# First layer of a two-block network: the pool's columns ahead of the recurrence, and the inverse in one pass over eight chunks

## The chip, the cores and the metric

The kernel runs on one core of a Trainium2 chip. The metric is the device time of one execution in microseconds (us). The engines are PE (TensorE, matmuls; PEld is its weight load), DVE (VectorE), ACT (ScalarE), POOL (GpSimd) and SP (SyncE, which issues most of the DMAs).

## The reference

Two blocks of a network over 256 tokens (and 256 context tokens) of width 2048. The change lies in layer 0 of the first block, where latent and context tokens, 512 rows in all, pass one projection `w_in` and are split: a pooling part, three vectors r, k, v for a recurrence with 16 heads of 64 in both directions, two small inputs for decay and a, and a gate.

```python
def wkv7_scan(state, inputs, reverse):
    def step(S, xs):
        r, w, k, v, a, b = xs
        sa = jnp.einsum('bhvk,bhk->bhv', S, a)
        S = S * w[:, :, None, :] + sa[..., None] * b[:, :, None, :] + v[..., None] * k[:, :, None, :]
        return S, jnp.einsum('bhvk,bhk->bhv', S, r)
...
def even_mixer(hl, hc, w_in, w_out, pool_w, pool_scale, ...):
    al, rl, kl, vl, wdl, adl, gl = split_even(hl @ w_in)
    ac, rc, kc, vc, wdc, adc, gc = split_even(hc @ w_in)
    for d, reverse in enumerate((False, True)):
        in_c = rwkv_dir_inputs(rc, kc, vc, wdc[..., d, :], adc[..., d, :], *dir_p, reverse)
        in_l = rwkv_dir_inputs(rl, kl, vl, wdl[..., d, :], adl[..., d, :], *dir_p, reverse)
        s_ctx, y_c = wkv7_scan(s0, in_c, reverse)
        _, y_l = wkv7_scan(s_ctx, in_l, reverse)
        outs_l.append(rwkv_readout(y_l, in_l, r_k, gn_g[d], gn_b[d]))
        ...
    ol = (outs_l[0] + outs_l[1]).astype(hl.dtype)
    yl = (jnp.concatenate([multiscale_pool(al, pool_w, pool_scale), ol], -1) * jax.nn.silu(gl)) @ w_out
```

The kernel computes the recurrence in chunks of 64 tokens. In each chunk the dependence of the tokens on each other is a triangular 64x64 system, whose inverse is found by doubling (five levels) and two refining steps; then a chain over the eight chunks carries the state.

## The kernel before

**Layer 0 in three kinds of work.** The *dense* work is `hX @ w_in`, in columns of 128 output features: 48 columns, each of 16 blocks of 128 inputs, each block a triple of matmuls 128x512 (L486 high part by high part, L487 high by low, L488 low by high), since float32 is split into two parts. `atoms` (L480) issues a column one triple at a time. Its weights come in two pieces of 512 KB a column (`need`, L835; `stream`, L466), each split in two halves into `whi` (ACT, L187) and `wlo` (DVE, L188). A column is one of r, k, v of a head pair (`rkv`), a gate (`gate`) or half of a pool group (`pool`). `poolmix` (L564) multiplies the pooled features by small weights (L571). *Side* work of the same queue is `mod` (L346), the modulation vectors, with four matmuls in a go at L369.

The *inverse*: there are 16 units, 8 head pairs p times 2 directions d. `wkv_prep` (L577) makes a unit's inputs. `wkv_half(u, g)` (L660) does chunks 4g to 4g+3 of both heads: masked copies S (the tile called STK in the code), the A matmuls (L692), DVE's masking of their result (L693, L701, L702), the subtraction at L695 and a cast on ACT (AT16, L697), and then steps of the form "eight 64x64 matmuls into the bank iv (`units`, L708), then one DVE operation out of that bank": x (L720, L746), t (L737, L750), y (L739, L752), each of 128x256. It also makes the transposed rows BT, UV, ZV (L724 to L734).

The *chain*: `wkv_chain(u, g)` (L756) goes through four chunks in three steps each: L770 on PE, R on DVE (L772); L776 on PE, UV on ACT (L777); L780 on PE, ZV on DVE (L783), with L784 and L785 on PE into the bank yb. `wkv_read` (L795) normalises the result, with the sums at L798 and L805.

**What sets the order.** PE's order is the order of the code (it is set by hand there); the other engines' order is a scheduler's, which takes the inverse's operations with priority 100 and the chain's with 60. `merge` (L911) writes the code order: each round takes one step of the inverse of one half, 0.75 steps of the chain of the half before, one step of prep and read, and then `fill`: as many dense triples (0.64 each by the planner's own unit) as keep the remaining dense work even over the remaining steps (`left`, `steps`, 575 in all). A unit goes through two merges: the inverse of its second half beside the chain of its first, and the inverse of the next unit's first half beside the chain of its second. `filler` (L869) hands out the columns in order, one entry of mod after nine triples. In the last unit, out-projection columns take the place of the dense ones.

## Time and profile before

| | us |
|---|---|
| time, median of 3 runs | 3622.39 |
| lowest and highest | 3620.04, 3637.42 |
| the profiled execution's own time | 3619.65 |
| its span in the profile | 3617.8 |
| PE busy in it | 3478.3 |
| DVE busy | 2240.6 |
| ACT busy | 1606.1 |

The mean granted clock of TensorE is 0.987 of its full 2.4 GHz. Layer 0's stage runs from about 299 to 1592 us. "Busy" on PE counts each matmul until its modelled end, and matmuls overlap, so the distance between two starts tells more of what one costs than its duration. An idle time in brackets, as in "[1.16 <-DVE R L772]", is the time in which the engine did nothing before this instruction, with what ended it.

### The profile page before, as it was taken

How to read it: one execution, taken by the hardware profiler on the slowest of the kernel's cores; microseconds unless marked ns; L12 is line 12 of the kernel's file. 1: busy time of each engine (PE TensorE's matmuls, PEld its weight loads, DVE VectorE, ACT ScalarE, POOL GpSimd, SP SyncE). 2: the span in 40 equal slices, each digit the busy share in tenths (PEclk: the TensorE clock that was granted, in tenths of full speed). 3: DMA queues.
4: the chain of work that ended last, by engine and by line, in shares of the span. 5: the costliest groups of instructions: out<-in, count | busy, mean ns of one | idle time of the engine just before them, and what ended most of it. 6: DMA issues, size and time to landing. Idle time of an engine off the chain costs nothing.

```text
span 3617.8 us, 56804 instructions
## 1 busy us (share of the span) xinstructions
PE 3478.3 (96%) x22385; PEld 2678.4 (74%) x22385; DVE 2240.6 (62%) x4180; ACT 1606.1 (44%) x2680; POOL 83.3 (2%) x168
## 2 busy tenths in 40 slices
PE   6999999999999999999999999999999999999998
PEld 4576666666666666678788887777888888888886
DVE  4253666777776777843656667766654566666544
ACT  3244344444444444431545555364444544444433
POOL 1000000000000000100000000000000000000000
PEclk9999999999999999999999999999999999999999
DMA  9976433344343344443444456454665566666654
GB/s 312 311 260 182 138 109 116 115 128 122 106 134 116 112 127 120 125 151 110 131 122 128 138 178 208 129 139 117 184 180 164 181 189 190 190 189 191 201 190 162
DMA packets 655652, 578.57 MB, mean 160 GB/s; under 512 B 24891, under 2 KB 498415, under 8 KB 655386
## 3 DMA queue, kind: packets, MB, share of 16 engines
q1 hardware_dynamic: 627008, 538.86, 49.9%
q10 hardware_dynamic: 24474, 29.09, 2.4%
q0 software_dynamic: 3904, 7.01, 0.7%
q8 instruction: 175, 2.87, 0.3%
q14 instruction: 91, 0.75, 0.1%
HBM read 547.32 MB, written 27.56 MB: 159 GB/s over the span
## 4 chain that ended last, share of the span: by engine, by line
issue 58%; PE 17%; DVE 3%; ACT 2%; DMA 1%; POOL 0%; ACTq 0%; POOLq 0%; SPq 0%; DVEq 0%
PE acc L486 3%; PE iv L708 3%; PE acc L487 2%; PE acc L488 2%; DMA raw<-ev_w_in 1%; PE acc L369 1%; PE ch L776 1%; PE ch L780 1%; PE sc L692 1%; PE ch L770 1%; PE yb L784 1%; PE yb L785 0%; DVE S L701 0%; ACT whi L187 0%; PE sc L724 0%
## 5 line engine op out<-in xcount | busy, mean ns | idle before, releaser
L188 DVE TENSOR_TENSOR wlo<-raw,whi 128x1024 fp32r<-128x1024 f32 (+1 forms) x857 | 928.2, 1088 | 813.2 <-ACT whi L187 806.7
L187 ACT CAST whi<-raw 128x1024 fp32r<-128x1024 f32 (+1 forms) x857 | 799.6, 940 | 1051.3 <-PE acc L207 212.2
L207 PE MATMUL acc<-A,whi 128*128 128x512 f32 x1488 | 531.6, 398 | 3.9 <-DVE A L1000 2.8
L208 PE MATMUL acc<-A,wlo 128*128 128x256 f32 x1488 | 424.2, 285 | 0.8 <-DVE wlo L188 0.8
L486 PE MATMUL acc<-A,whi 128*128 128x512 f32 x768 | 359.2, 468 | 22.8 <-ACT ev L497 14.2
L207 PEld LDWEIGHTS acc<-A,whi 128*128 128x128 f32 x1488 | 278.5, 187 | 68.3 <-DVE A L1000 3.1
L487 PE MATMUL acc<-B,whi 128*128 128x512 f32 x768 | 303.3, 395 | 0.0
L488 PE MATMUL acc<-A,wlo 128*128 128x512 f32 x768 | 302.0, 393 | 0.0
L208 PEld LDWEIGHTS acc<-A,wlo 128*128 128x128 f32 x1488 | 281.1, 189 | 5.1 <-DVE wlo L188 1.8
L207 PE MATMUL iv<-A,whi 128*128 128x512 f32 x736 | 257.5, 391 | 0.0
L208 PE MATMUL iv<-A,wlo 128*128 128x256 f32 x736 | 206.3, 280 | 1.0 <-DVE wlo L188 1.0
L486 PEld LDWEIGHTS acc<-A,whi 128*128 128x128 f32 x768 | 145.8, 190 | 81.9 <-issue 32.3
L488 PEld LDWEIGHTS acc<-A,wlo 128*128 128x128 f32 x768 | 144.8, 189 | 33.3
L487 PEld LDWEIGHTS acc<-B,whi 128*128 128x128 f32 x768 | 146.3, 191 | 22.0 <-issue 9.6
L207 PEld LDWEIGHTS iv<-A,whi 128*128 128x128 f32 x736 | 137.7, 187 | 30.3
L208 PEld LDWEIGHTS iv<-A,wlo 128*128 128x128 f32 x736 | 139.1, 189 | 1.5 <-DVE wlo L188 1.5
L720 DVE TENSOR_TENSOR x<-iv,k 128x256 f16<-128x256 f32 x160 | 67.4, 421 | 90.3 <-PE iv L708 88.4
L777 ACT COPY UV<-ch 64x128 f32<-64x128 f32 x128 | 33.3, 260 | 186.6 <-PE ch L776 182.0
L708 PEld LDWEIGHTS <-at 64*64 64x64 f16 x1536 | 40.4, 108 | 91.5 <-issue 75.6
L708 PEld LDWEIGHTS <-y 64*64 64x64 f16 x1536 | 40.1, 108 | 82.4 <-issue 50.6
L737 DVE TENSOR_TENSOR t<-iv,t 128x256 f16<-128x256 f32 x128 | 54.0, 422 | 48.2 <-PE iv L708 46.0
L776 PE MATMUL ch<-R,Y 128*128 128x128 f32 x256 | 63.3, 330 | 14.2 <-DVE R L772 14.0
(1540 smaller groups left out, 7136.3 us busy)
## 6 DMA issues: line engine op xcount, KB each, us to landing
raw<-w_gate_up SPq DMA_DIRECT2D x176, 512.0 KB, 4.7
raw<-mod_w SPq DMA_DIRECT2D x128, 512.0 KB, 4.0
raw<-ev_w_in SPq DMA_DIRECT2D x100, 512.0 KB, 4.6
raw<-w_down SPq DMA_DIRECT2D x88, 512.0 KB, 4.9
raw<-od_w_in SPq DMA_DIRECT2D x80, 512.0 KB, 3.7
raw<-w_in SPq DMA_DIRECT2D x80, 512.0 KB, 4.0
raw<-w_xkv SPq DMA_DIRECT2D x64, 512.0 KB, 6.6
A<-mod_w SPq DMA_DIRECT2D x64, 512.0 KB, 5.9
```

Of the source, the lines that this page charges most:

```text
L187: nc.scalar.copy(hi[:, q], raw[:, q])
L188: nc.vector.tensor_sub(lo[:, q], raw[:, q], hi[:, q].bitcast(F32))
L207: s.nc.tensor.matmul(acc, hi, x.rearrange("p a t -> p (a t)"), start=start, stop=False)
L208: s.nc.tensor.matmul(acc[:, 0:256], lo, x[:, 0], start=False, stop=stop)
L369: nc.tensor.matmul(acc[32 * q:32 * q + 32], s.SC[:, 2 * k:2 * k + 32], pair[q // 2][:, q % 2], start=k < 4, stop=k >= 12, tile_position=(0 ...
L486: s.nc.tensor.matmul(acc, hi[:, k], hX[kx], start=kx == 0, stop=False)
L487: s.nc.tensor.matmul(acc, hi[:, k], lX[kx], start=False, stop=False)
L488: s.nc.tensor.matmul(acc, lo[:, k], hX[kx], start=False, stop=kx == 15)
L708: nc.tensor.matmul(ps[hs[h], c], l(hs[h], c), r(hs[h], c), start=True, stop=True)
L720: tt(X16, px, b4(s.lv[d][l]), MUL)
L737: tt(T16 if l < 5 else T32, pt, T16, ADD)
L776: nc.tensor.matmul(pr[:, 128:256], fl(Y32[:, b:b + 2]), R1, start=True, stop=True)
```

## The change

**The pool first, in full pieces.** `rkv(0)` and then, for the four pool groups, two pool columns, two gates and the poolmix are queued first: 19 dense columns, with no `mod` among them. What of them is not used up in the first unit's prep is drained in one go before the first inverse, with pieces of 512 KB as before. 29 columns are left (`later`): r, k, v of the other head pairs and eight gates.

**Smaller pieces after that.** The room for weights is shared from then on: `small_stream` brings each column in four pieces of 256 KB (`kper` 4), through two raw halves and two halves each of `whi` and `wlo`, unsplit. The other three raw tiles hold mod's two pieces and the inverse's AT and T32; the other pair of `whi` and `wlo` holds S of every second unit (`s.S2`).

**The inverse over eight chunks.** `wkv_inv(u, e)` replaces the two `wkv_half`: each call of `units` is sixteen 64x64 matmuls (L741), each DVE operation out of it 128x512 (x L748, L756; T, Y L749, L753, L758). The masking is done for each half (L726, L730, L731), S only on its 64x256 part and AB over all 128 partitions, so that the fill of AB's lower part on POOL is gone. `wkv_rows` holds the transposes.

**The chain as the frame.** `wkv_chain` has 24 steps for a unit; `merge` takes one chain step in a round, 0.75 steps of the next unit's inverse, the prep of the unit after that (two units ahead) and the read of the one before, and then dense triples, over 18 + 24 x 15 steps. The read has two empty steps instead of six. The sum of both directions is taken up in prep (L675 to L677) instead of the read.

```diff
+    def small_stream(s, srcs, raws, his, los):
+
+        nc, loaded, got = s.nc, [0], {}
+
+        def get(i):
+            while loaded[0] < min(i + 3, len(srcs)):
+                j = loaded[0]
+                if j >= 2:
+                    split(j - 2)
+                nc.sync.dma_start(raws[j % 2], srcs[j])
+                loaded[0] += 1
+            for j in range(i, min(i + 2, len(srcs))):
+                split(j)
+            return got[i]
+
+        def split(j):
+            if j in got:
+                return
+            hi, lo = got[j] = his[j % 2], los[j % 2]
+            nc.scalar.copy(hi, raws[j % 2])
+            nc.vector.tensor_sub(lo, raws[j % 2], hi.bitcast(F32))
+        return get
+
...
-        for q in range(2):
+        for q in range(16 // s.kper):
             hi, lo = s.wget(i + q)
-            for k in range(8):
-                kx = 8 * q + k
+            for k in range(s.kper):
+                kx = s.kper * q + k
...
-        nc.vector.tensor_tensor(u.OUT, ps, V, MUL)
+        if d == 0:
+            nc.vector.tensor_tensor(u.OUT, ps, V, MUL)
+        else:
+            rk = s.T("tb", [P, 512])
+            nc.vector.tensor_tensor(rk, ps, V, MUL)
+            nc.vector.tensor_tensor(u.OUT, u.OUT, rk, ADD)
...
+        for g in range(2):
+            cs = slice(4 * g, 4 * g + 4)
+            pss = []
+            for h in range(2):
+                ps = s.PS("sc", (P, 4, 2, C))
+                for c in range(4):
+                    nc.tensor.matmul(ps[:, c], fl(u.BK)[:, 4 * g + c], u.S[g][:, c, :, h], start=True, stop=True)
+                tt(AT[hs[h], cs], ps[0:64, :, 0], b4(mk[0:64, 0:64], 64), MUL)
+                pss.append(ps)
+            yield 1
+            for h, ps in enumerate(pss):
+                tt(u.S[g][osd[h], :, 0, h], ps[64:128, :, 0], b4(mk[64:128, 0:64], 64), MUL)
+                tt(u.AB[g][:, :, h], ps[:, :, 1], b4(mk[:, 64:128], P), MUL)
+        tt(AT, AT, b8(s.id64), SUB)
+        AT16 = s.T("inv", [P, NCH, C], F16)
         nc.scalar.copy(AT16, AT)
...
         def units(l, r):
-            ps = s.PS("iv", (P, 4, C))
-            for c in range(4):
+            ps = s.PS("iv", (P, NCH, C))
+            for c in range(NCH):
                 for h in range(2):
                     nc.tensor.matmul(ps[hs[h], c], l(hs[h], c), r(hs[h], c), start=True, stop=True)
             return ps
...
+            tt(X16, px, b8(s.lv[d][l]), MUL)
...
+    def wkv_rows(s, u, g):
+
+        nc, hs, osd, C = s.nc, s.hs, s.osd, CH
+        fl = lambda t: t.rearrange("p c a t -> p c (a t)")
+        UV, ZV, BT = (s.T("%s%d" % (n, g), [P, 4, 2, C]) for n in ("UV", "ZV", "BT"))
...
+        ps = s.PS("sc", (P, 4, 128))
+        for c in range(4):
+            nc.tensor.transpose(ps[:, c], fl(u.BH[g])[:, c], s.ident)
+        nc.scalar.copy(fl(BT), ps)
+        u.h[g] = (UV, ZV, BT)
+
+    def wkv_chain(s, u, nxt, before):
+
...
+            if g == 0:
+                for x in before:
+                    for _ in x:
+                        pass
...
+            if g == 0 and nxt is not None:
+                s.wkv_rows(nxt, 0)
...
-        for _ in range(6):
+        for _ in range(2):
...
         nc.vector.tensor_tensor(OUT, OUT, YS, ADD)
-        if d == 0:
-            s.fwd = OUT
-        else:
-            nc.vector.tensor_tensor(OUT, OUT, s.fwd, ADD)
+        if d == 1:
+            s.await_gate(8 + p)
...
+        s.kper = 8
         rkv(0)
-        for p in range(8):
-            if p < 7:
-                rkv(p + 1)
-            if p in (2, 4, 6):
...
-        mods = [s.mod(0, 8, 12), s.mod(1, 0, 12)]
...
+        for g in range(4):
+            pool(g)
+            gate(2 * g)
+            gate(2 * g + 1)
+            jobs.append(s.l0_poolmix(g))
+        dense, dsrcs = jobs[:], srcs[:]
+        del jobs[:], srcs[:]
+
+        def later():
+            s.kper = 4
+            rkv(1)
+            for p in range(2, 8):
+                rkv(p)
+                gate(6 + p)
+            gate(14)
+            gate(15)
...
-                    if n % 9 == 0:
+                    if n * 80 // 464 > (n - 1) * 80 // 464:
...
-        steps = [575.0]
+        steps = [18.0 + 24 * 15]
...
         def merge(a, b, side):
-            na, nb, done = 16.0, 12.0, 0.0
...
+            due = 0.25
+            while a is not None or b is not None:
+                due += 0.75 if b is not None else 1.0
+                if a is not None and due >= 1.0:
+                    due -= 1.0
                     with s.prio(100):
-                        w = next(a, s)
-                    a, more = (a, True) if w is not s else (None, more)
-                    w = 1.0 if w is s else w
...
+                        if next(a, None) is None:
+                            a = None
+                if b is not None:
                     with s.prio(60):
-                        b, more = (b, True) if next(b, s) is not s else (None, more)
...
-                steps[0] = max(steps[0] - w, 1.0)
-                fill(w * left[0] / steps[0])
+                steps[0] = max(steps[0] - 1.0, 1.0)
+                fill(left[0] / steps[0])
...
         cur, pg = prep(0)
         for _ in pg:
             fill(1.5)
-        merge(s.wkv_half(cur, 0), None, [])
+        for _ in F:
+            pass
+
+        later()
+        raw = [s.T("raw", [P, 1024], bufs=s.nraw) for _ in range(4)]
+        r2 = raw[2].rearrange("p (n k c) -> p n k c", n=2, k=4)
+        s.AT, s.T32 = [raw[3][:, i * 512:(i + 1) * 512].rearrange("p (c t) -> p c t", c=NCH) for i in range(2)]
+        wh = [s.T(t, [P, 2, 4, 128], F32R, bufs=s.nhi) for t in ("whi", "wlo")]
+        s.S2 = [s.T(t, [P, 4, 2, 2, CH], bufs=s.nhi) for t in ("whi", "wlo")]
+        s.wget = s.small_stream(srcs, [r2[:, 0], r2[:, 1]], [wh[0][:, 0], wh[0][:, 1]], [wh[1][:, 0], wh[1][:, 1]])
+        F = filler([r.rearrange("p (k c) -> p k c", k=2) for r in raw[0:2]])
+        credit[0], left[0] = 0.0, 29 * 16 * 0.64 + 16 * (4 * 0.6 + 0.9)
+        nxt, pg = prep(1)
+        merge(s.wkv_inv(cur, 1), None, [pg])
+        s.wkv_rows(cur, 0)
         rg = []
         for n in range(16):
-            nxt, pg = prep(n + 1) if n < 15 else (None, iter(()))
-            merge(s.wkv_half(cur, 1), s.wkv_chain(cur, 0), rg + [pg])
+            s.wkv_rows(cur, 1)
+            nx2, pg = prep(n + 2) if n < 14 else (None, iter(()))
             if n == 15:
                 for _ in F:
                     pass
                 s.out0 = F = s.l0_out_n(0)
-                credit[0], left[0], steps[0] = 0.0, 18, 14.0
-            merge(s.wkv_half(nxt, 0) if nxt else None, s.wkv_chain(cur, 1), [])
+                credit[0], left[0], steps[0] = 0.0, 26, 24.0
+            merge(s.wkv_inv(nxt, n % 2) if nxt else None, s.wkv_chain(cur, nxt, rg), rg + [pg])
             rg = [s.wkv_read(cur)]
-            cur = nxt
+            cur, nxt = nxt, nx2
         for _ in rg[0]:
             fill(1.3)
```

What stands in a row on the engines, before and after. First PE in the steady middle of the stage, before: two rounds of the inverse, with the names iv<-t,at for x's matmuls, iv<-x,y and iv<-y,x for those of t and y. A row of L708 stands for eight such pairs of weight load and matmul, the rest of which are left out.

```order
L486 MATMUL acc<-A_1572,whi 128x512
L487 MATMUL acc<-B_1580,whi 128x512
L488 MATMUL acc<-A_1572,wlo 128x512
L708 LDWEIGHTS at_11856
L708 MATMUL iv<-t_11894,at_11856 64x64
...
L770 MATMUL ch<-ZV_11364,S_11354 128x128
L486 MATMUL acc<-A_1572,whi 128x512
L487 MATMUL acc<-B_1580,whi 128x512
L488 MATMUL acc<-A_1572,wlo 128x512
L486 MATMUL acc<-A_1573,whi 128x512
...
L708 LDWEIGHTS y_11895
L708 MATMUL iv<-x_11896,y_11895 64x64
```

After, the same kind of place; L741 is the inverse's line now, L819 to L824 the third step of the chain, and a row of L741 stands for sixteen pairs.

```order
L509 MATMUL acc<-A_1571,whi 128x512
L510 MATMUL acc<-B_1579,whi 128x512
L511 MATMUL acc<-A_1571,wlo 128x512
L369 MATMUL acc<-raw,SC 32x512 x4
L741 LDWEIGHTS T_12125
L741 MATMUL iv<-Y_12126,T_12125 64x64
...
L741 LDWEIGHTS Y_12126
L741 MATMUL iv<-T_12125,Y_12126 64x64
...
L819 MATMUL ch<-UV_11560,BT_11562 128x128
L823 MATMUL yb<-S_11134,ZV_11561 128x128
L824 MATMUL yb<-AB_11150,UV_11560 128x128
L509 MATMUL acc<-A_1571,whi 128x512
```

What moved: a round of the inverse has twice the matmuls, and the stretches of chain and dense work between rounds are no longer in the middle of four chunks.

Second, DVE at the head of an inverse, before: after the A matmuls the two AT parts (L693), S (L701), AB (L702), the subtraction (L695), then the chain's R (L772).

```order
L693 TENSOR_TENSOR AT<-sc,k_65 64x256
L701 TENSOR_TENSOR S_8902<-sc,k_65 64x8x64
L693 TENSOR_TENSOR AT<-sc,k_65 64x256
L702 TENSOR_TENSOR AB_8914<-sc,k_65 64x4x64
L695 TENSOR_TENSOR AT<-AT,id_83 128x256
L701 TENSOR_TENSOR S_8902<-sc,k_65 64x8x64
L702 TENSOR_TENSOR AB_8914<-sc,k_65 64x4x64
L716 TENSOR_TENSOR y_8988<-at_8954,k_1528 128x256
L772 TENSOR_TENSOR R_8961<-ch,k_65 128x128
L715 TENSOR_TENSOR t_8987<-iv,k_1528 128x256
```

After, with AT in a tile named raw (L726), S (L730) and AB (L731), for the second half of the unit; between the first half's such rows and these the chain's ZV (L822) now has its place.

```order
L822 SCALAR_TENSOR_TENSOR ZV_5807<-ZV_5807,We,ch 64x64 x2
L726 TENSOR_TENSOR raw<-sc,k_65 64x256
L730 TENSOR_TENSOR S_6237<-sc,k_65 64x4x64
L731 TENSOR_TENSOR AB_6249<-sc,k_65 128x4x64
L726 TENSOR_TENSOR raw<-sc,k_65 64x256
L730 TENSOR_TENSOR S_6237<-sc,k_65 64x4x64
L731 TENSOR_TENSOR AB_6249<-sc,k_65 128x4x64
L732 TENSOR_TENSOR raw<-raw,id_83 128x512
L811 TENSOR_TENSOR R_6347<-ch,k_65 128x128
```

What moved: the masking of a unit stands in two parts around the chain's ZV, the subtraction (L732) comes once and is 128x512, and R follows the second part.

Third, PE late in the stage, where no dense triples are left, before: an inverse of the last unit beside the chain of the unit before.

```order
L776 MATMUL ch<-R_17653,Y_17200 128x128
L805 MATMUL sc<-sq,k_65 128x512
L708 LDWEIGHTS at_17560
L708 MATMUL iv<-t_17573,at_17560 64x64
...
L780 MATMUL ch<-UV_17148,BT_17150 128x128
L784 MATMUL yb<-S_17139,ZV_17149 128x128
L785 MATMUL yb<-AB_17151,UV_17148 128x128
L708 LDWEIGHTS y_17574
L708 MATMUL iv<-x_17575,y_17574 64x64
...
L708 LDWEIGHTS x_17575
L708 MATMUL iv<-y_17574,x_17575 64x64
```

After, at the same unit: sixteen pairs in a row of L741; L781 and L789 are the transposes of `wkv_rows`.

```order
L781 MATMUL sc<-k_65,m_15267 128x128 x2
L789 MATMUL sc<-k_65,BH 128x128 x4
L809 MATMUL ch<-ZV_15926,wlo 128x128
L815 MATMUL ch<-R_16237,pw 128x128
L741 LDWEIGHTS T_16043
L741 MATMUL iv<-Y_16044,T_16043 64x64
...
L741 LDWEIGHTS Y_16044
L741 MATMUL iv<-T_16043,Y_16044 64x64
...
L819 MATMUL ch<-UV_15925,BT_15927 128x128
L823 MATMUL yb<-wlo,ZV_15926 128x128
L824 MATMUL yb<-pv_15243,UV_15925 128x128
L741 LDWEIGHTS inv
```

What moved: from the last dense triple (L486, L509) to the first out-projection matmul PE has 12 chain steps and 17 inverse groups before (and the last poolmix entries), 34 chain steps and 21 groups after.

Counted over all of PE's order: groups of 64x64 matmuls that stand together, 478 before and 240 after; runs of dense matmuls that stand together, 480 before and 338 after; poolmix entries, sixteen of one and four of four.

## Rows read from the trace of the kernel before

**Rows 1.** The page: span, and busy time of each engine.

```profile
span 3617.8 us, 56804 instructions
PE 3478.3 (96%) x22385; PEld 2678.4 (74%) x22385; DVE 2240.6 (62%) x4180; ACT 1606.1 (44%) x2680; POOL 83.3 (2%) x168
```

**Rows 2.** Busy time by stretch: stretch, length, PE, PEld, DVE, ACT, POOL, clock, DMA.

```profile
376.00:1511.00 1135.00, 1086.31 (x10229) 750.12 (x10227) 818.91 (x1975) 483.85 (x1011) 55.27 (x111) 1.00 0.39 118
1511.00:1556.00 45.00, 34.14 (x385) 25.38 (x384) 35.97 (x82) 21.39 (x41) 3.71 (x7) 0.77 0.61 199
```

**Rows 3.** Timeline of PE: start, duration (us), instruction, tiles, shapes.

```profile
1254.06 0.31 PE L708 MATMUL iv<-x,y 64*64 64x64 f16 x8
1254.20 0.29 PE L708 MATMUL iv<-y,x 64*64 64x64 f16 x8
1254.42 0.50 PE L486 MATMUL acc<-A,whi 128*128 128x512 f32 x1
1254.76 0.39 PE L487 MATMUL acc<-B,whi 128*128 128x512 f32 x1
1254.99 0.39 PE L488 MATMUL acc<-A,wlo 128*128 128x512 f32 x1
1255.31 0.31 PE L708 MATMUL iv<-t,at 64*64 64x64 f16 x8
1255.55 0.49 PE L770 MATMUL ch<-ZV,S 128*128 128x128 f32 x2
```

**Rows 4.** Waits of PE, 340 to 1590 us: us in total, times, longest.

```profile
PE ch L776 <- DVE R L772: 14.0, 15, 1.3
...
PE iv L708 <- ACT at L697: 8.1, 5, 3.8
PE iv L708 <- DVE t L737: 6.5, 10, 2.1
...
PE iv L708 <- DVE x L720: 4.6, 8, 1.1
```

**Rows 5.** Timeline of the head of one inverse.

```profile
1048.98 0.28 DVE L772 TENSOR_TENSOR R<-ch,k 128x128 f32<-128x128 f32 x1
...
1049.31 0.49 PE L776 MATMUL ch<-R,Y 128*128 128x128 f32 x2 [1.16 <-DVE R L772]
```

**Rows 6.** DVE by line, 340 to 1590 us: count, busy, mean ns, idle before.

```profile
L188 DVE TENSOR_TENSOR wlo<-raw,whi 128x512 fp32r<-128x512 f32 x190 | 127.0, 684 | 40.7 <-ACT whi L187 39.7
L720 DVE TENSOR_TENSOR x<-iv,k 128x256 f16<-128x256 f32 x160 | 67.4, 421 | 90.3 <-PE iv L708 88.4
...
L737 DVE TENSOR_TENSOR t<-iv,t 128x256 f16<-128x256 f32 x128 | 54.0, 422 | 48.2 <-PE iv L708 46.0
...
L649 DVE TENSOR_TENSOR op<-sc,vs 128x512 f32<-128x512 f32 x16 | 11.0, 685 | 3.3 <-PE sc L648 3.1
```

**Rows 7.** Timeline of PE, late stretch without dense triples.

```profile
1511.56 0.31 PE L708 MATMUL iv<-t,at 64*64 64x64 f16 x8 [0.21 <-DVE t L737]
...
1515.26 0.49 PE L780 MATMUL ch<-UV,BT 128*128 128x128 f32 x2
...
1516.03 1.02 PE L571 MATMUL acc<-pv,pw 128*128 128x512 f32 x2
...
1529.97 0.42 PE L708 MATMUL iv<-id,at 64*64 64x64 f16 x8 [3.85 <-ACT at L697]
...
1539.18 0.49 PE L780 MATMUL ch<-UV,BT 128*128 128x128 f32 x2 [0.75 <-ACT UV L777]
...
1555.17 0.79 PE L770 MATMUL ch<-ZV,S 128*128 128x128 f32 x2
1555.61 0.77 PE L1048 MATMUL acc<-whi,A 128*128 128x512 f32 x1
```

**Rows 8.** ACT by line, same columns; and the page's DMA issues (KB, us to landing).

```profile
L187 ACT CAST whi<-raw 128x512 fp32r<-128x512 f32 x190 | 111.6, 617 | 106.0 <-DMA raw<-ev_w_in 43.4 <-PE acc L487 40.5 <-PE iv L1050 8.5
...
raw<-ev_w_in SPq DMA_DIRECT2D x100, 512.0 KB, 4.6
```

More of the change, by code (lines that the diff above doesn't have):

```diff
@@ L344, in mod_prep, with mod @@
         s.gsc = [s.dpool.tile([2, 2048], F32, tag="g%d" % l, name="g%d" % l) for l in range(2)]
-    def mod(s, l, j0, j1, ring=None):
+    def mod(s, cols, ring, bank):
         nc, I = s.nc, s.I
-        lst = [(j, kc) for j in range(j0, j1) for kc in range(8)]
+        lst = [(l, j, kc) for l, j in cols for kc in range(8)]
         got = {}
@@ L360, in mod @@
         for i in range(0, len(lst), 2):
-            j, kc = lst[i]
-            for q in range(2 if ring is None else 8):
+            l, j, kc = lst[i]
+            for q in range(len(ring)):
                 load(i + q)
             if kc == 0:
-                acc = s.PS("acc" if ring is None else "iv")
+                acc = s.PS(bank)
             pair = [got.pop(i), got.pop(i + 1)]
@@ L378, in mod @@
             yield 0.6
-            ps = s.PS("acc" if ring is None else "iv")
+            ps = s.PS(bank)
             if j < 8:
@@ L682, in wkv_half @@
+        for g in range(2):
+            cs = slice(4 * g, 4 * g + 4)
+            BH = s.T(("BH", "cat")[g], [P, 4, 2, C])
+            tt(fl(BH), fl(u.BK)[:, cs], We[:, cs].broadcast_to([P, 4, 2 * C]), MUL)
+            u.BH.append(BH)
+            u.AB.append(s.T(("AB0", "AB1", "pu", "pv0")[2 * e + g], [P, 4, 2, C]))
         yield 1
-        AT = s.T("AT", [P, 4, C])
+        AT, T32 = s.AT, s.T32
         mk = s.m2[d]
-        b64 = lambda a: a[:, None, :].broadcast_to([64, 4, a.shape[1]])
@@ L687, in wkv_half @@
-        b4 = lambda a: a[:, None, :].broadcast_to([P, 4, C])
-        pss = []
-        for h in range(2):
-            ps = s.PS("sc", (P, 4, 128))
-            for c in range(4):
-                nc.tensor.matmul(ps[:, c].rearrange("p (a t) -> p a t", a=2), fl(u.BK)[:, 4 * g + c], STK[:, c, :, h], start=True, stop=True)
-            tt(AT[hs[h]], ps[0:64, :, 0:64], b64(mk[0:64, 0:64]), MUL)
-            pss.append(ps)
-        tt(AT, AT, b4(s.id64), SUB)
-        AT16 = s.T("at16", [P, 4, C], F16)
@@ L795, in wkv_read @@
+        s.dump("wkvy%d" % d, u.YS, lambda o: o[u.p])
     def wkv_read(s, u):
@@ L837, in need @@
             for c in cols:
[L838 to L839 removed]
+                for k in range(16 // s.kper):
+                    w = W[k * s.kper * P:(k + 1) * s.kper * P, c:c + 128].rearrange("(k p) c -> p k c", p=P)
+                    srcs.append((w, s.kper, 128) if s.kper == 8 else w)
             return i
@@ L878, in filler @@
                 yield c
-        F = filler()
+        F = (c for job in dense for c in job)
         left = [45 * 16 * 0.64 + 16 * 0.86 + 16 * (4 * 0.6 + 0.9)]
@@ L937, in merge, with await_gate @@
                     pass
+        def await_gate(f):
+            while f not in s.have_gate:
+                fill(0.6)
+        s.await_gate = await_gate
         cur, pg = prep(0)
@@ L1589, in head @@
         mem = (x for f in range(16) for x in s.mem_k(f))
-        mod = s.mod(0, 0, 8, ring=ring)
+        mod = s.mod([(0, j) for j in range(8)], ring, "iv")
         for i, _ in enumerate(s.mem_kv()):
```

186 lines of the change are left out of this document (74 added, 112 removed).

## The prediction

> **What bounds the kernel now.** I read the page's totals first: TensorE is busy for 3478.3 of 3617.8 us [rows 1], so time is saved by giving PE less to do or fewer gaps, and a shorter operation elsewhere counts only where PE waits for it. The profiled execution took 3619.65 us, 2.7 below the median of the runs (3622.39); my sum is made against 3619.65. Then I read the stretches. From 376 to 1511 us PE has 48.7 us without work out of 1135 [rows 2]; from 1511 to 1556, where dense columns have run out, it has 10.9 out of 45, and its clock was granted at 0.77 of the upper level. The layer's stage, some 299 to 1592 us, is all that the change touches.
>
> "Busy" hides the main thing: what the hops between kinds of matmul cost. For that I read starts in a clean piece of the steady stretch, not durations [rows 3]. Dense matmuls start 0.23 us apart (1254.76, 1254.99). The last one before an inverse group takes 0.32 until the group starts (0.09 lost), and the first one after a group takes 0.34 (0.11 lost). A group of eight 64x64 matmuls takes 0.24 (1255.31 to 1255.55), two groups in a row take 0.36 (1254.06 to 1254.42): so 0.12 for each further eight, and a fixed 0.12 for each time that PE turns to the inverse. A dense triple alone takes 0.89 (1254.42 to 1255.31), where 3 x 0.23 would be 0.69.
>
> **The change part by part.** It neither adds nor removes matmuls of the inverse, the chain, the dense columns or the modulation to speak of; it puts them in larger pieces. I counted contiguous pieces in the order of PE.
>
> Inverse: 478 groups become 240, since eight chunks go in one call instead of four. 238 x 0.12 = **-28.6 us**.
>
> Dense: 480 runs become 338, most of that because 19 columns now run solid before the first inverse. 142 x (0.09 + 0.11) = **-28.4 us**. The solid columns themselves move and cost nothing: a piece of 512 KB feeds 24 matmuls, 5.5 us at 0.23; it lands in 4.6 us and is loaded ahead, and its split takes two halves of 0.62 on ACT and 0.68 on DVE [rows 6, 8]. Should one of these lag, each of the 38 pieces costs the difference.
>
> The Trainium skill ("TensorEngine Tiling (Array Packing)", Key Properties) says that a change of tiling mode makes TensorE drain. The rows agree in kind: a dense matmul lasts 0.39 and frees the next start after 0.23, so a full drain would lose 0.16 on each side, and 0.09 and 0.11 are seen. By the full drain the two terms would be 238 x 0.32 = 76 instead of 57, and the time 19 us less than my forecast. I keep to the starts.
>
> Heads of units: after the A matmuls DVE has a burst of masking, and R1 of the chain stands behind it. One such place shows PE idle 1.16 us for R [rows 5]; in all PE waits 14.0 us, 15 times, for R and 8.1 us for the inverse's first operand, AT16, 3.8 of that in the late stretch that I count below [rows 4, 7]. AT16 is now made once for eight chunks, and the burst stands in two parts with a chain step and dense triples between them. I take half of 14.0 + 4.3: **-9 us** (bounds 0 and -18).
>
> Evacuation: a DVE operation after each inverse group now has 512 columns for 256, 0.685 instead of 0.42 us, by the row of a 128x512 subtraction or product out of PSUM [rows 6]; so 0.264 later for whoever waits. Nobody waiting, it costs 0; all 240 groups waiting, 240 x 0.264 = 63. Now PE waits 18 times for x or t, of 288 such operations [rows 4, 6], about one in 16, since a dense triple or a chain step lies between. That cover stays: 464 triples over 378 steps follow 768 over 575, and there are now 1.33 chain steps for each inverse step instead of 0.75. I take a tenth of the groups: 24 x 0.264, with rounding up **+7 us**. The sum of DVE's work falls, as half as many operations share their fixed cost and the 64x512 mask goes; DVE is not the bound, so I count that at nothing.
>
> The end without filling: before, from 1511.56 to 1555.61, 44.1 us hold 12 chain steps and 17 inverse groups with next to no dense work [rows 7]. By clean prices that is some 22 us of matmuls (chain steps 3 to a chunk, with 0.77 for the three pairs of the third, 1515.26 to 1516.03, and an estimated 0.3 for each of the others; groups at 0.24 to 0.36; the A matmuls, transposes, sums and two poolmix entries the rest): 22 us of waiting. After, the order leaves 34 chain steps and 21 groups there, some 33 us by the same prices. At the pace of before by chain steps, (1555.17 - 1539.18)/7 = 2.3 us, that lasts 78 us; by groups, 44.1/17 = 2.6, it lasts 55. Waiting is then 45 or 22, which is 23 or 0 more than now. Wider evacuations and a chain that is now the frame speak for the upper part: **+14 us**.
>
> Nothing for the rest, each with its cover: the AB fill on POOL goes (POOL has 83.3 us of work in all [rows 1]); the read has four empty yields less; OUT is summed in prep, one 0.685 operation in a pair's prep, under dense triples; poolmix goes from sixteen entries of one to four of four, 12 x 0.2, some 2 us gained at most; bias and modulation keep their number. Prep two units ahead fetches the next heads' inputs earlier, which only takes waits away.
>
> Sum: -28.6 - 28.4 - 9 + 7 + 14 = -45, so 3619.65 - 45 = **3575 us**.
>
> **The rivals.** *The evacuation paces the inverse.* The next group of the inverse needs the whole of the last one, evacuated. If each group waits the full 0.264, the 7 becomes 63: 3575 + 56 = 3631 us, no change to speak of. For it: DVE is idle 88.4 us waiting for PE before x [rows 6], so the two take turns; against it: PE itself rarely waits at that place [rows 4]. The Trainium skill (same page, PSUM Bottleneck) states that packing speeds up TensorE but not the emptying of PSUM, which may become the limit; the rows of before show PE waiting 11.1 us in all for x and t, so the trace bears it out little so far.
>
> *Slower: the small weight ring.* After the pool stage 29 columns come in 116 pieces of 256 KB through two raw halves and two hi/lo halves. A half can be split only when PE has left the piece before the last. If PE catches up with it, each piece costs up to a split that nobody hides, 0.617 on ACT and 0.684 on DVE [rows 6, 8], 1.30 in all: 116 x 1.30 = 151, and 3726 us. The gain is gone at 45/116 = 0.39 us per piece and the time is over 0.5% longer than before from 0.54; half of the price gives 3650. Against it: a piece feeds four triples, at one or two triples between chain steps some 9 us, and the load that takes 4.6 us for twice the bytes is issued a piece ahead. For it: where ACT or DVE is in a burst at a head, the split queues behind.
>
> *More gain.* Of PE's 48.7 us without work in the long stretch I take 9. If longer pieces cover most of the rest, 40 more go: 3535 us. For it: those waits are many and short. Against it: some are column edges and first loads that stay.
>
> That the change doesn't do what it says is ruled out by the order, which shows the pieces as told.
>
> **How the numbers follow.** Forecast 3575, with its own range 3540 to 3608 (terms at their bounds, the fall of the evacuation excepted), chance 0.50. More gain 0.20. Evacuation 0.17. Small ring 0.13. The range 3510 to 3640 takes in the first three but for the tail of more gain, and leaves out most of the small ring. Faster by over 0.5% (about what a measurement of this kernel can tell; below 3604) is the forecast and more gain: 0.70. Within it 0.17. Slower 0.13.
>
> **What would show it.** In the trace of after: inverse groups at a start distance of 0.36 for sixteen, and the same 0.09 and 0.11 at their sides; DVE at about 0.685 for x and t, with PE waiting for them in a few groups only (a mean of over 0.2 us a group is the first rival); PE's waits for R and AT16 halved; a solid piece of some 210 us (19 x 48 x 0.23) with dense starts 0.23 apart; and a stretch of 55 to 78 us without dense work before the out-projection, at a clock below 1. PE waiting for whi or wlo of the small pieces is the second rival. I am wrong if PE's idle time in the stage grows by more than 57 us, whichever engine it waits for.

## The result: slower by one per cent

| | before | after |
|---|---|---|
| time, median, us | 3622.02 (4 runs) | 3669.41 (4 runs) |
| lowest and highest | 3620.04, 3637.42 | 3661.04, 3677.84 |
| ratio, 95% interval | | 1.0113 [1.0095, 1.0131] |
| span of the profiled execution | 3617.8 | 3659.3 |

The forecast was 3575 us, in a range of 3510 to 3640. The time went the other way and out of the range, and the prediction's own sign of being wrong came: PE's idle time in the stage grew by more than 57 us (63.4, below). The page of after answers to [rows 1]:

```profile
span 3659.3 us, 56514 instructions
PE 3455.7 (94%) x22385; PEld 2701.6 (74%) x22385; DVE 2189.3 (60%) x3813; ACT 1637.9 (45%) x2661; POOL 67.4 (2%) x136
```

PE is busy for 23 us less in a span that is 42 us longer: the work fell, the gaps grew. Where, the stretches tell, as [rows 2]: the pool's columns until the first inverse (298 to 544.5), the stretch with inverse, chain and dense work, the stretch after the last dense triple, and the out-projection. The columns are the stretch, its length, then PE, PEld, DVE, ACT, POOL, the clock and the DMA.

```profile
298.00:544.50 246.50, 237.45 (x1010) 186.86 (x1010) 115.78 (x207) 81.28 (x141) 2.85 (x6) 0.99 0.40 119
544.50:1531.80 987.30, 879.54 (x9182) 619.19 (x9182) 669.01 (x1430) 452.52 (x871) 37.28 (x75) 0.96 0.39 121
1531.80:1591.80 60.00, 47.74 (x693) 38.81 (x691) 45.02 (x93) 26.45 (x58) 4.26 (x8) 0.86 0.38 117
1591.80:1781.60 189.80, 188.67 (x850) 153.38 (x848) 73.31 (x105) 48.16 (x63) 1.08 (x2) 1.00 0.40 124
```

I split each stretch into three: time in which PE has no work (length less PE busy), time lost to the clock (length times one less the clock) and the rest, PE's work at the full 2.4 GHz. The clock is printed to a hundredth, so for the sums I took its loss in windows of 10 us, where the rounding hardly counts. For before I used the four stretches that lie between the same events.

```profile
299.00:380.60 81.60, 73.41 (x336) 50.12 (x335) 34.90 (x66) 32.12 (x53) 0.31 (x1) 0.96 0.62 188
380.60:1511.00 1130.40, 1082.68 (x10209) 748.19 (x10205) 814.65 (x1966) 481.78 (x1007) 55.27 (x111) 1.00 0.39 118
1511.00:1555.60 44.60, 33.74 (x384) 24.98 (x383) 35.56 (x81) 21.33 (x41) 3.71 (x7) 0.77 0.61 197
1555.60:1739.70 184.10, 184.10 (x807) 149.68 (x807) 69.52 (x93) 41.37 (x51) 1.08 (x2) 0.99 0.38 123
```

| sum of the four stretches, us | before | after | difference | forecast |
|---|---|---|---|---|
| PE's work at the full clock | 1353.5 | 1300.6 | -52.9 | -57 |
| PE without work | 66.8 | 130.2 | +63.4 | +12, with the clock |
| lost to the clock | 20.4 | 52.8 | +32.4 | |
| length | 1440.7 | 1483.6 | +42.9 | -45 |

The forecast of the work is right as a sum. What undoes it are 60 us more of waiting in the second stretch (107.8 where it was 47.7) and a clock of 0.96 there instead of 1.00. The waits of PE in the whole stage, as [rows 4] (total, times, longest):

```profile
PE sc L625 <- DVE pv L731: 25.2, 15, 4.4
PE sc L625 <- DVE AB L731: 18.2, 12, 2.7
PE sc L841 <- ACT ZV L786: 17.5, 15, 1.4
PE ch L809 <- DVE ZV L822: 16.7, 14, 3.0
PE acc L509 <- ACT ev L520: 12.4, 8, 4.7
PE ch L815 <- DVE R L811: 7.2, 6, 3.1
PE iv L741 <- DVE Y L753: 6.7, 11, 2.6
```

L625 is the first matmul of a unit's prep, L841 the read's first sum. Both need one of the two banks called sc, which the A matmuls (L725) and the transposes (L781, L789) fill just ahead of them; L731 is the last of the masks that empty it. In before the same two matmuls (L618, L798) wait 2.4 us in all:

```profile
PE sc L618 <- ACT tb L610: 1.8, 4, 0.6
PE sc L798 <- ACT YS L791: 0.6, 1, 0.6
```

R's 7.2 us answer to 14.0 there, and AT16's 8.1 us have no row any more [rows 4].

What a head looks like (start, duration, engine, instruction, and in brackets the idle time before it and what ended it; rows of other engines and of the dense triples are left out):

```profile
1077.01 1.28 ACT L849 ACT_TABLE_LOAD   x1 [3.63 <-PE sc L848]
1078.30 0.69 ACT L849 ACTIVATE sq<-sc,eps 128x512 f32<-128x512 f32 x1
1078.65 1.95 PE L725 MATMUL sc<-wlo,BK 128*128 128x128 f32 x16
1079.01 1.28 ACT L851 ACT_TABLE_LOAD   x1
1080.30 0.63 ACT L851 ACTIVATE sq<-sq 128x512 f32<-128x512 f32 x1
1080.43 0.39 PE L809 MATMUL ch<-ZV,S 128*128 128x128 f32 x2
...
1080.96 0.69 DVE L853 TENSOR_TENSOR YS<-YS,sq 128x512 f32<-128x512 f32 x1 [3.47 <-ACT sq L851]
1081.57 0.69 DVE L500 TENSOR_TENSOR wlo<-raw,whi 128x512 fp32r<-128x512 f32 x1
...
1082.29 0.42 DVE L726 TENSOR_TENSOR raw<-sc,k 64x256 f32<-64x256 f32 x1
...
1083.16 0.42 DVE L731 TENSOR_TENSOR pv<-sc,k 128x256 f32<-128x256 f32 x1
...
1083.73 0.47 PE L625 MATMUL sc<-TW,m 128*128 128x512 f32 x1 [2.91 <-DVE pv L731]
```

DVE's queue holds the read's multiplication L853 ahead of the masks. It waits for ACT, which loads two tables and computes, so DVE does nothing for 3.47 us, in which the A matmuls fill both banks (they end at 1080.60). L853 and a split of a weight piece (L500) come next, and only from 1082.29 on the masks; PE has issued one chain matmul and stands at L625 for 2.91 us. And the clock falls behind it:

```profile
1081.00:1084.90 3.90, 0.71 (x2) 0.30 (x2) 3.77 (x9) 1.68 (x3) 0.00 (x0) 1.00 0.63 221
1084.90:1088.30 3.40, 3.22 (x9) 2.68 (x10) 3.31 (x7) 1.17 (x4) 0.53 (x1) 0.50 0.00 0
1088.30:1092.00 3.70, 3.70 (x35) 2.79 (x34) 1.76 (x5) 3.00 (x6) 0.00 (x0) 1.00 0.01 2
```

In the first piece PE works 0.71 of 3.90 us, in the second it is busy at a granted clock of 0.50, which is the lower level of 1.2 GHz, in the third it is back at 2.4.

### The profile page after: what moved, and what is told of

It is laid out like the page before. It is cut to its first block, busy times and chain, and to the rows that moved or that the text cites. A ratio compares the mean times of both kernels' runs of the same rounds, so it can differ in the third digit from the quotient of the medians.

```text
span 3659.3 us, 56514 instructions
## 1 busy us (share of the span) xinstructions
PE 3455.7 (94%) x22385; PEld 2701.6 (74%) x22385; DVE 2189.3 (60%) x3813; ACT 1637.9 (45%) x2661; POOL 67.4 (2%) x136
## 4 chain that ended last, share of the span: by engine, by line
issue 59%; PE 27%; DVE 5%; ACT 3%; DMA 2%; POOL 0%; ACTq 0%; SPq 0%; DVEq 0%; POOLq 0%
PE acc L509 4%; PE acc L510 4%; PE acc L511 4%; PE iv L741 3%; PE acc L369 2%; PE ch L815 1%; PE acc L207 1%; PE ch L819 1%; DMA sgT<-ev 1%; PE ch L809 1%; PE sc L725 1%; PE yb L823 1%; PE yb L824 0%; PE acc L1627 0%; PE acc L1628 0%
## 5 line engine op out<-in xcount | busy, mean ns | idle before, releaser
L188 DVE TENSOR_TENSOR wlo<-raw,whi 128x1024 fp32r<-128x1024 f32 (+2 forms) x742 | 850.9, 1150 | 850.6 <-ACT whi L187 845.5
L187 ACT CAST whi<-raw 128x1024 fp32r<-128x1024 f32 (+2 forms) x742 | 732.2, 990 | 1060.0 <-PE acc L207 209.7
L509 PE MATMUL acc<-A,whi 128*128 128x512 f32 x768 | 353.0, 460 | 18.5 <-ACT ev L520 12.4
L207 PEld LDWEIGHTS acc<-A,whi 128*128 128x128 f32 x1488 | 277.9, 187 | 66.8 <-DVE A L1059 1.8
L509 PEld LDWEIGHTS acc<-A,whi 128*128 128x128 f32 x768 | 149.4, 195 | 84.7 <-issue 35.8
L500 DVE TENSOR_TENSOR wlo<-raw,whi 128x512 fp32r<-128x512 f32 x116 | 80.0, 689 | 70.1 <-ACT whi L499 69.1
L499 ACT CAST whi<-raw 128x512 fp32r<-128x512 f32 x116 | 71.6, 617 | 112.2 <-PE acc L510 105.3
L822 DVE SCALAR_TENSOR_TENSOR ZV<-ZV,We,ch 64x64 f32<-64x64 f32 x224 | 62.0, 277 | 35.4 <-PE ch L819 33.0
L224 PE MATMUL acc<-whi,B 128*128 128x512 f32 x192 | 76.7, 401 | 0.0
L225 PE MATMUL acc<-wlo,B 128*128 128x512 f32 x192 | 75.8, 395 | 0.2 <-DVE wlo L188 0.2
```

The source lines that it names most:

```text
L187: nc.scalar.copy(hi[:, q], raw[:, q])
L188: nc.vector.tensor_sub(lo[:, q], raw[:, q], hi[:, q].bitcast(F32))
L207: s.nc.tensor.matmul(acc, hi, x.rearrange("p a t -> p (a t)"), start=start, stop=False)
L224: nc.tensor.matmul(acc, xh, hi[:, kk], start=k == 0, stop=False)
L225: nc.tensor.matmul(acc, xh, lo[:, kk], start=False, stop=False)
L500: nc.vector.tensor_sub(lo, raws[j % 2], hi.bitcast(F32))
```

## The experiments

The theory after this reading: heads of units lose the time, since four users take the banks sc one after the other while DVE's queue is blocked, and the dense triples that could cover it have been moved into the pool stage. Rivals: the small weight ring, the wide evacuations, or the pool-first order by itself.

**The pool first, alone.** The kernel before with the new order of columns and the spacing of `mod` that goes with it; inverse, chain and weight pieces are as before.

```diff
         rkv(0)
-        for p in range(8):
...
+        for g in range(4):
+            pool(g)
+            gate(2 * g)
+            gate(2 * g + 1)
+            jobs.append(s.l0_poolmix(g))
+        dense = jobs[:]
...
+        for _ in F:
+            pass
+        F = filler()
...
         merge(s.wkv_half(cur, 0), None, [])
```

> The kernel before, with the first part of the change alone: 19 columns with the pool first and drained in one go, then the 29 others; inverse, chain, read and weight pieces as before. Theory (the loss comes from the heads of the units, where matmuls wait for the bank sc): the heads are those of before, so this gains what 480 to 359 dense runs are worth, 121 x 0.20 = 24 us, less a dry stretch of 25 chain steps for 12 (some 10 to 15 us): 3600 to 3615. Rival (the loss comes from the dense work being too thin beside the inverse after the pool is done): 3640 or more, with PE idle in many places of the steady stretch, not at the heads.

3709.68 us, ratio 1.023 [1.0191, 1.0269]. This half of the change alone costs 86 us, where I had expected a gain; the rest of the change wins 40 of them back. The stretch with the inverse:

```profile
540.80:1608.00 1067.20, 954.46 (x9623) 654.74 (x9622) 759.55 (x1862) 443.40 (x933) 55.51 (x111) 0.96 0.37 116
```

PE is without work for 112.7 us there and the clock is 0.96. The waits are those of before, grown: AT16 (L697) 38.8 us for 8.1, R 18.1 for 14.0, t (L737) 12.9 for 6.5 [rows 4]. By the same split over the four stretches PE's work is only 1.4 us less than in before, for 121 dense runs fewer; the clock loses 40.8 us.

**The cover given back.** The same kernel, with 304 of the later triples issued twice.

```diff
                 yield 0.64
+                s.nd += s.twice
+                if s.nd >= 1.0 and kx < 15:
+                    s.nd -= 1.0
+                    s.nc.tensor.matmul(acc, hi[:, k], hX[kx], start=False, stop=False)
+                    s.nc.tensor.matmul(acc, hi[:, k], lX[kx], start=False, stop=False)
+                    s.nc.tensor.matmul(acc, lo[:, k], hX[kx], start=False, stop=False)
+                    yield 0.64
```

> e1_pool_first with 304 of its later dense triples issued twice, dealt out evenly, so that the rounds beside the inverse have as many dense triples as in the kernel before (768); the second issue adds the same product again, so it computes something else and does 304 x 0.69 to 0.89 = 210 to 270 us more work on PE. Theory (the first part of the change loses since it takes the dense cover away from the rounds): idle time in the steady stretch falls from 113 to 50 to 65 us and the clock's loss from some 40 to 5 to 15 us, time 3710 + 240 - 80 = 3830 to 3890. Rival (the loss has another cause, the order of columns or the loads): idle time stays at 100 or more, 3920 to 3980.

3828.68 us: 119 more than the pool first, for at least 304 x 0.69 = 210 us of added work.

```profile
534.70:1734.50 1199.80, 1137.74 (x10525) 791.66 (x10525) 761.74 (x1860) 444.49 (x933) 55.07 (x111) 0.99 0.33 104
```

PE is without work for 62.1 us, and the clock is 0.99. Four tenths of the added work were free, since it filled waits and kept the clock up. So most of what the pool-first order loses is the dense cover beside the inverse; the order of the columns has no other fault of that size. It is not a return to before in full: the trace counts 761 triples in this stretch, where before has 687 in its own and waits 47.7 us.

**The read's place.** The changed kernel with the read's empty steps of before. In the first of two versions the last unit's read is late too, so that the out-projection reads its last input before it is written; the second mends that, and a temporary of the gate takes the read's own tile. The second version's edit:

```diff
-        th = s.T("rn", [P, 512])
+        th = s.T("sq" if f >= 8 else "rn", [P, 512])
...
-        for _ in range(2):
+        for _ in range(2 if (p, d) == (7, 1) else 6):
             yield
```

> The changed kernel with six empty yields in the read again, as before, and nothing else. Theory A (DVE's queue is blocked at the head by the read's multiplication, which waits for ACT, and the masks stand behind it): the wait of L625 for the masks falls from 43 us to under 25, the clock in the steady stretch rises, time 15 to 40 us less, some 3635. Theory B (the masks alone are long enough to keep the bank sc): waits as they are, within 8 us of the changed kernel.

> The changed kernel with six empty yields in the read, the last unit's read excepted (in e2_read6 the out-projection read its last input too early, which this mends; the gate's temporary shares the read's own tile). Theory: the time of e2_read6, 3610 to 3625: PE's idle time in the steady stretch some 20 us and the half clock some 35 us lower than in the changed kernel, since DVE's masks no longer stand behind the read's multiplication. Rival (e2_read6 was only shorter for the early out-projection): 3650 to 3670.

3616.98 us, ratio 0.9985 [0.9968, 1.0001], for the first; 3630.72 us, 1.0009 [0.9993, 1.0025], for the second, against 1.0113 for the change. Shortening the read, which I had counted at nothing, costs about 1%. In the mended version DVE stands at L853 for 8.9 us, 4 times, where it stood 38.4 us, 13 times. L625 waits 21.7 us instead of 43.4, and the stretch with the inverse has 87.2 us without work at a clock of 0.98. The wait for ZV (L822) grew to 25.2.

**Prep later, alone.**

```diff
+        for _ in range(4):
+            yield
+
         L = s.T("ss", [P, 512])
```

> The changed kernel with four empty yields in the prep ahead of its first matmuls, so that L625 no longer follows the A matmuls of the next unit. Theory (PE stands at L625 since both banks of sc are in use by the masks): L625's 43 us of waits go almost wholly, and part of the 40 us that the lower clock costs: 3600 to 3625. Rival (small weight pieces and wide evacuations hold PE back, and the wait at L625 only shows where): another wait takes its place, 3650 to 3670.

3660.96 us, ratio 1.0114 [1.0088, 1.014]: nothing gained. The theory's first form was too simple. L625 waits no more, but

```profile
PE ch L818 <- DVE R L814: 66.6, 28, 4.5
```

the chain's R, which stands behind the masks in DVE's queue, takes its place (the whole stage; L814 is L811 of after). While DVE is blocked, PE stops at whichever instruction next needs DVE.

**Prep and read later, together**, with the chain still behind the inverse in each round (and the last read late, as in the first version above):

```diff
+        for _ in range(6):
+            yield
+
         L = s.T("ss", [P, 512])
...
+        for _ in range(5):
+            yield
         ps = s.PS("sc")
         nc.tensor.matmul(ps, s.blk, YS, start=True, stop=True)
```

> The changed kernel with prep's first matmuls six steps later and the read's first sum five steps later, so that transposes, A matmuls, read and prep take the bank sc one after the other. Theory: L625's 43 us, L841's 17 us and half of the chain's 17 us of waits go, and most of the half clock with them: 3560 to 3595, below the kernel before. Rival: as for the prep alone, 3640 to 3670.

3623.61 us, ratio 0.9997 [0.9981, 1.0013]: better than the change, short of what was expected. R still waits 28.2 us, and prep's own sum now waits 23.0 us for the copies (L789 there) of the next transposes.

**The chain ahead of the inverse.** The second read version with the two halves of a round exchanged in the code.

```diff
+                if b is not None:
+                    with s.prio(60):
+                        if next(b, s) is s:
+                            b = None
                 if a is not None and due >= 1.0:
                     due -= 1.0
                     with s.prio(100):
                         if next(a, None) is None:
                             a = None
-                if b is not None:
-                    with s.prio(60):
-                        if next(b, s) is s:
-                            b = None
```

> e5_read6_ok, and in each round of merge the chain's step is written ahead of the inverse's step instead of behind it, so that R and ZV enter DVE's queue ahead of the masks of the same round. Theory A (the order in DVE's queue decides who waits at a head): PE's waits for R and ZV, 30 us in e2_read6, fall to under 12, time 10 to 25 us under e5_read6_ok. Rival B (the burst on DVE is paid in some place whatever the order): another wait grows by as much, within 8 us of e5_read6_ok.

3618.38 us, ratio 0.998 [0.9962, 0.9999], 12 us under its base (their intervals just overlap). The wait for ZV fell from 25.2 to 2.5 us; R rose from 8.1 to 13.8. Theory A holds for the time; the two waits together fell from 33.3 to 16.3 us, not under the 12 expected.

**More dense triples at the heads**, fewer elsewhere; then with the chain first as well.

```diff
-            due = 0.25
+            due, rnd, heavy = 0.25, 0, b is not None and a is not None
...
-                steps[0] = max(steps[0] - 1.0, 1.0)
-                fill(left[0] / steps[0])
+                rnd += 1
+                w = (2.0 if rnd <= 7 else (24.0 - 14.0) / 17) if heavy else 1.0
+                steps[0] = max(steps[0] - w, 1.0)
+                fill(w * left[0] / steps[0])
```

> e5_read6_ok with the dense triples dealt out unevenly: twice the share in the first seven rounds of a unit, 0.59 of it in the other seventeen. Theory B (what a head lacks is independent work for PE): idle time in the steady stretch falls from 87 to 50 to 65 us, with it the half clock, and the time by 15 to 40 us to 3575 to 3600. Rival (cover is short everywhere): the waits move to the later rounds (x, y, ZV), within 8 us of e5_read6_ok.

> e6_chain_first and e7_fill_heads together. If both causes are real and separate the gains add: 3560 to 3590, below the kernel before. If they remove the same waits: no lower than the better of the two.

3652.89 us, ratio 1.0073 [1.0047, 1.01], and 3662.04 us, 1.0097 [1.0068, 1.0126]. A miss: both are slower than their bases. L625 hardly gains (18.9 us for 21.7), and the thinner rounds lose: PE is without work for 111.6 us in the stretch with the inverse, against 87.2, with the wait for Y (L753) at 13.0 us for 2.8. Cover is not short at the heads alone; taken from other rounds it costs more there.

**The users of sc apart.** The chain first, the read's sums at rounds 6 and 8, prep's matmuls at round 7. Between the read's sums there are two empty steps again, as in the change; the exchange of the two halves of a round is not shown a second time.

```diff
+        for _ in range(3):
+            yield
+
         L = s.T("ss", [P, 512])
...
+        for _ in range(0 if (p, d) == (7, 1) else 5):
+            yield
         ps = s.PS("sc")
         nc.tensor.matmul(ps, s.blk, YS, start=True, stop=True)
```

> e6_chain_first, with the read's first sum at round 6 and its second at round 8 and prep's first matmuls at round 7, so that transposes, A matmuls, read and prep use the two banks sc one after the other. Theory: the waits of L841 for ACT's copies (15 us) and of L625 for the masks (22 us) go without a new one, since the chain now stands ahead of the masks: idle time in the steady stretch from 75 to about 40 us, time 30 to 45 us under e6_chain_first, 3575 to 3590. Rival (as with the prep alone: the wait only moves): within 10 us of e6_chain_first.

3585.79 us, ratio 0.9878 [0.9849, 0.9908]: as expected, and below the kernel before. The stretch with the inverse, and the longest waits of the whole stage:

```profile
543.70:1458.00 914.30, 851.04 (x9192) 626.59 (x9192) 667.60 (x1432) 448.78 (x873) 36.68 (x76) 0.98 0.41 130
```

```profile
PE acc L509 <- ACT ev L520: 16.0, 9, 6.7
PE ch L818 <- DVE R L814: 15.0, 21, 2.4
PE ch L822 <- ACT UV L819: 12.7, 17, 2.7
```

The waits for a bank sc come to 3.3 us in all. PE is without work for 63.3 us where the change has 107.8; some 40 were expected, and ACT's late copies of finished columns (L520) and of UV (L819) now lead.

**Where the dense work ends.** The last version with the planner's remaining work counted 20 units lower, so that the triples last to the out-projection; and, on the kernel of the next paragraph, 25 units higher. The first of the two edits:

```diff
-        credit[0], left[0] = 0.0, 29 * 16 * 0.64 + 16 * (4 * 0.6 + 0.9)
+        credit[0], left[0] = 0.0, 29 * 16 * 0.64 + 16 * (4 * 0.6 + 0.9) - 20.0
```

> e9_sc_apart with the planner's remaining dense work counted 20 units lower, so that the dense triples are dealt out more thinly and last to the out-projection. Theory (the stretch without dense work at the end costs its waits and the half clock, about 16 + 12 us): the end gains 10 to 25 us and the steady stretch, a little thinner, loses 0 to 10: 5 to 20 us under e9_sc_apart. Rival (cover is short everywhere, what the end gains the middle loses): within 5 us.

> e11_cast_dve with the planner's remaining dense work counted 25 units higher, the reverse of e10_dense_last: denser rounds first, and dense work ends earlier. Theory (waits grow faster than in proportion as cover gets thinner): within 8 us of e11_cast_dve to 15 us less, since the middle loses fewer waits than the end gains. Rival (an even spread is best): 15 to 30 us more.

3620.84 us, ratio 0.9982 [0.9961, 1.0003], 35 us longer than its base; and 3589.95 us, 0.9897 [0.9877, 0.9917], 21 us longer than its base. Both directions lose. Thinner triples cost the middle more than the end without dense work costs; denser ones lengthen that end to 118 us at a clock of 0.80.

**The small pieces cast on DVE.**

```diff
-            nc.scalar.copy(hi, raws[j % 2])
+            nc.vector.tensor_copy(hi, raws[j % 2])
```

> e9_sc_apart with the high part of each small weight piece made by DVE instead of ACT, so that DVE's subtraction never stands waiting for ACT (69 us of such idle time on DVE in the changed kernel), at 116 x some 0.4 to 0.7 us more work on DVE. Rival of the prediction (the small weight ring holds things up, by way of DVE's queue): PE's idle time falls by 15 us or more and the time with it. Theory (the heads do): DVE's added 50 to 80 us make heads worse, 0 to 30 us longer than e9_sc_apart.

3568.9 us, ratio 0.9842 [0.9816, 0.9869]: the best kernel of the study, 53 us under before and 17 under its base (their intervals overlap). The theory said the opposite sign; the rival was right about the direction, at 8.7 us less of waiting (its 15 were not reached) and a clock of 0.99 for 0.98.

```profile
535.50:1438.80 903.30, 848.71 (x9191) 625.41 (x9192) 704.41 (x1546) 388.06 (x760) 37.34 (x76) 0.99 0.42 131
```

In the change DVE stands still for 69.1 us, 58 times, waiting for ACT's cast before it can subtract (L500), with masks, R and ZV behind it in its queue. But in the base only 28.2 us of that are left, and here DVE stands as long at the cast, until PE has left the half of `whi`:

```profile
DVE wlo L500 <- ACT whi L499: 28.2, 25, 3.2
DVE whi L499 <- PE acc L510: 27.1, 25, 3.7
```

DVE does 37 us more work (704.41 for 667.60), and ACT does 61 less (388.06 for 448.78). Over the whole stage PE's waits for ACT's copies fall: L520 from 16.0 to 13.6, UV from 12.7 to 9.5, L539 from 8.5 to 6.8. That points to the relief of ACT and not to DVE's wait; no run separates the two.

**The mends without the change.** The kernel before, with the chain first and prep three rounds later.

```diff
+        for _ in range(3):
+            yield
+
         L = s.T("ss", [P, 512])
...
+                done += nb / na if a is not None else 1.0
+                while b is not None and done >= 1.0:
+                    done -= 1.0
+                    with s.prio(60):
+                        b, more = (b, True) if next(b, s) is not s else (None, more)
+                w = 1.0
                 if a is not None:
                     with s.prio(100):
...
```

> The kernel before, with the same two mends of the heads as in e9_sc_apart as far as they fit: the chain's step written ahead of the inverse's in each round, and prep's first matmuls three rounds later. Theory (at the heads of before dense work covers the masks, R excepted): R's 14 us of waits fall, some 5 to 12 us less than before, 3608 to 3618, so that most of the gain of e9_sc_apart is the change's own. Rival (the order in the queues is worth as much without the change): 3585 to 3600.

3646.29 us, ratio 1.0054 [1.0032, 1.0076]: worse than before. A miss for both theories. R's wait is gone from the long ones, but prep's sum (L605 there) now waits 18.3 us for the read's activation, and x 13.8 us for 4.6. So these two mends bring the kernel before nothing. The read's later first sum and the cast on DVE were not tried there.

## Why the prediction was wrong, point by point

**Fewer hops of PE: right as a sum, and that by luck.** 57 us were forecast, 52.9 measured. Groups of sixteen start about as expected (0.36 for sixteen):

```profile
1253.65 0.39 PE L511 MATMUL acc<-A,wlo 128*128 128x512 f32 x1
1253.96 0.44 PE L741 MATMUL iv<-Y,T 64*64 64x64 f16 x16
1254.24 0.42 PE L741 MATMUL iv<-T,Y 64*64 64x64 f16 x16
1254.59 0.49 PE L819 MATMUL ch<-UV,BT 128*128 128x128 f32 x2
```

0.31 into the group, 0.28 for sixteen, 0.35 to the chain. But the pool first alone, with 121 dense runs fewer, saved 1.4 us of work, where my price makes 24 of them. So the dense term was far too large and, if the two parts simply add, the inverse's far too small: some 50 us for 238 turns to the 64x64 form and back. Two wrong sizes made a right sum. By a full drain, which the Trainium skill ("TensorEngine Tiling (Array Packing)", Key Properties) speaks of, I had estimated 76 us; the measured 52.9 lie nearer to the 57 from the starts.

**Wide evacuations: an upper guess.** The operation takes 0.686 us (L756), as forecast, and PE waits 7 us for the whole inverse, where it waited 11.1 for x and t alone [rows 4]. So the +7 was some 11 too high, and that rival is out. The Trainium skill's warning of PSUM emptying (same page, PSUM Bottleneck) is not borne out for the inverse; the emptying that held PE up here is that of the A matmuls (43.4 us at L625).

**The end without dense work: right in length, wrong in its cost.** 60.0 us, in the forecast 55 to 78. But 39 us of it are work at the full clock, so waits and clock take 21, as much as before (44.6 less 23.5). The +14 was 0.

**Heads of units: the step that failed.** R's wait halved to 7.2 us and AT16's went, so what I priced there came. What I counted at nothing brought the loss: "the read has four empty yields less" and prep "only takes waits away". I costed these as work that moves under dense triples, and did not ask which bank and which queue they are moved past. The prep's first matmuls and the read's first sum now stand right behind the A matmuls at the two banks sc, and the read's multiplication stands ahead of the masks in DVE's queue. L625 and L841 wait 61 us together and the chain's next matmul another 17 for ZV, none of which was in the sum. Putting the read back brought 39 us, the chain ahead 12, and the read's first sum and prep apart from the masks 33, 84 in all; prep alone brought nothing.

**"That cover stays": wrong.** I compared triples per step, 464 over 378 with 768 over 575. The 768 take in 81 that went before the first inverse; the two stretches with the inverse have 458 and 687. Per step that is still no thinner. But what needs cover is DVE's and ACT's work, and that did not shrink with the steps: to each triple DVE has 1.46 us of work (669 to 458), where it had 1.19 (815 to 687), and ACT 0.99 for 0.70. The pool first alone shows what such thin cover costs, 86 us with the inverse as it was, and the cover given back shows that most of it is cover. No run has the new inverse with the old order of columns, so how the change's own loss divides between cover and heads stays open.

**The clock: left out.** The forecast speaks of a lower clock only for the end. In the stretch with the inverse it fell to 0.96; over the stage the clock lost 32 us more. Each microsecond of waiting there cost about half of one more.

**The rivals.** The second, the small ring, was placed at PE, and PE never waits for whi or wlo of a small piece. Something of it was real in another place: by casting on DVE 17 us came back, some 0.15 a piece, below the 0.39 at which it would have decided. No rival named the banks sc.

The mechanism that was meant to gain does gain: with its heads mended the change makes 3585.79 us, 37 us under the kernel before, and with the cast moved as well 3568.9, 53 us under it.

## What to carry to other kernels

When steps are moved in time, list for each the bank it takes and the queues it enters, and see who stands next to it there; "hidden under other work" is not enough. Work that is drained in one solid piece is cover taken from somewhere else: count cover against the work of the engines that it hides, not against steps. When PE waits in many short pieces, price the clock with the wait.

## What was not expected of the hardware

Behind the stop of 2.91 us shown above the granted clock stood at 0.50 for 3.4 us in which PE was busy again, so a short stop is paid for twice. In the stretch with the inverse the lower level held for some 83 us, in before for 10. Added matmuls were partly free: 210 us of them cost 119.

A cast of 128x512 from float32 takes 0.420 us on DVE (L499 of the run with the cast on DVE), where ACT takes 0.617 [rows 8].
